# Recurrent layer of a hybrid decoder: operand tiles of two blocks, chunk steps without GpSimd

## The chip, the cores and the metric

The kernel runs on one core of one Trainium2 chip. The metric is the device time of one execution in microseconds (us), lower is better. The engines are TensorE (PE, matmuls), VectorE (DVE), ScalarE (ACT), GpSimd (POOL) and SyncE (SP, which here only issues DMAs). SBUF is the on-chip memory, PSUM holds the results of matmuls.

## The reference

The program is a decoder of two layers on one sequence of 512 tokens with 1024 channels, all in float32. Layer 0 is sparse attention with an MLP; layer 1, which the change concerns, is an RWKV-7 mixer with an MLP. Cut to what matters:

```python
# per token t, 16 heads of 64 channels: r, w (decay), k, v, kk, b = kk * a
sa    = einsum('bhvk,bhk->bhv', state, -kk_t)
state = state * w_t + sa[..., None] * b_t + v_t[..., None] * k_t
y     = einsum('bhvk,bhk->bhv', state, r_t)
# after the scan, per head:
mean = mean(y); var = mean((y - mean)**2)
y = (y - mean) * rsqrt(var + LNX_EPS) * lnx_w + lnx_b
bonus = sum(r * k * r_k) * v
out = ((y + bonus) * g) @ w_o
```

## The kernel before, in words

Channels lie on partitions in 8 blocks of 128 (two heads each), tokens on the free axis. Large matmuls are made with operands split in a high and a low part (`hi`, `lo`, three products in `gemm`, lines 119 to 121); a weight block of 1 MB for two blocks is loaded to `wraw` by a DMA on SP (line 76) and split by ACT (line 93) and DVE (line 101).

The scan runs over 8 chunks of 64 tokens. Its stages in `rwkv`:

- *Middle* (m = 0 to 7): per block, `front` and `middle` make the chunk operands. `AR` holds for each block and chunk the pair (a, r), `KB` the pair (b, k); each is 4 tiles, two for chunks 0 to 3 and two for chunks 4 to 7, of four blocks each (`half(t, f)` is one half of the tokens). `back` makes the 64x64 matrices `Mt` of all chunks, `rhat` the r operand, `bonus` sums over a head. The r GEMMs run between them.
- *Inversion* (`invert`): the diagonal 32x32 blocks of all the chunks' matrices go through DRAM (`dn`) into `tn`, one matrix per partition and half f, and are inverted in 30 iterations, each a product and an add for each half (lines 1030, 1033). Then a transposed copy `tt`, stores to DRAM (`dm`, `dt`), and loads into `Mt` and `T11`. `invert` is a generator: it yields an estimate of cost, and `run(t)` takes pieces up to t; HOLD (1e9) ends a call.
- *v GEMM*: per weight block, with `run(RUNW)` in between; `vcopy` brings v to `VT`, one tile per four chunks.
- *Chunk steps* n = 0 to 7: `step_z` multiplies the operand AL and the state-and-value tile `SV` (line 1323) and copies to `Zb`; `step_u` multiplies by the inverse and copies into `SV`; `step_n` makes the next state (L1350, `st`, `sv` L1357, `Sb`, `sn`); `step_r` and `step_y` make the output. Beside them run, for the next chunk, `acopy` (a part of AL, GpSimd), `vload` (values into `SV`, GpSimd), `opnd` (masked products into AL and `BL`, transposes), `merge` (the off-diagonal part of the inverse), and for chunks before, `gnorm` (group norm) and `turn` (transposes). `vmean` takes the mean of v beforehand, and `vload` subtracts it. The gate GEMM (`g2`), the split of the layer's output (`out`) and the output projection (`wo`) are pulled in at written places (`fill`).

Large tiles come from one pool of 21 slots (tag `b8`); a slot is free when the last reader of its tile is done. A planner orders the instructions of each engine by their place in the program and by priorities (`PR`, a number of places by which a site is put earlier; `gnorm` has 200, `step_u` 400, `acopy` 400, `vload` -100, `step_r` -1000) and its own costs. In the loop of chunk steps PE is taken out of it: `manual_schedule` keeps PE's instructions as written. Each engine executes its queue in order.

Of the kernel before, what the change touches and what calls it, by code (L numbers as in the profile page):

```python
# [765 lines left out]
def rwkv(c, x, ks, gi):  # L766
# [155 lines left out]
    KB, Mt = [[], []], []  # L922
    pc = c.tmp.tile([128, KC, NCH], F32, name="pc", tag="pc", bufs=1)

    def kb(f, m, s):
        return KB[f][m // 4][:, m % 4, :, s]
# [3 lines left out]
    pbo = pb[:, 0, :64].rearrange("p (n a e) -> p n a e", n=NCH, e=2)  # L930

    @c.site("front")
    def front(m):
# [20 lines left out]
    def middle(m):  # L954
        if m % 4 == 0:
            for f in range(2):
                KB[f].append(c.b8("KB", F32, (128, 4, 4, 2, 64)))
# [15 lines left out]
        for f in range(2):  # L973
            nc.vector.scalar_tensor_tensor(kb(f, m, 0), half(bt, f), 0.5, half(iP, f), op0=OP.mult, op1=OP.mult)
        for f in range(2):
            k4 = half(kk, f)
            nc.vector.scalar_tensor_tensor(ar(f, m, 0)[:, :, 1:], k4[:, :, 1:], -1.0, ar(f, m, 1)[:, :, :63],
                                           op0=OP.mult, op1=OP.mult)
            nc.scalar.activation(ar(f, m, 0)[:, :, 0:1], k4[:, :, 0:1], AF.Copy, scale=-1.0)
# [27 lines left out]
    def invert():  # L1007
# [37 lines left out]
        yield HOLD  # L1045
# [54 lines left out]
    nc.vector.tensor_copy(bo, pbo.rearrange("p n a e -> p n (a e)"))  # L1100
# [8 lines left out]
    def sl(t, n, q):  # L1109
        return t[n // 4][q // 4][:, q % 4, n % 4]  # L1110
# [69 lines left out]
    def opl(n, j):  # L1180
# [18 lines left out]
        for e in range(2):  # L1199
            mask((j, 1, e), BL[n][:, e, js, 0:64], pl[:, e, :, 1], kon[:, None, 1].to_broadcast([128, 4, 64]))  # L1200
# [429 lines left out]
```

## Time and profile before

| | |
|---|---|
| times of three runs | 1377.22, 1379.87, 1380.18 us (median 1379.87) |
| profiled execution | 1377.53 us, span 1375.4 us |
| granted TensorE clock, mean | 0.972 |
| PE busy | 1298.9 us (94%), 8237 instructions |
| DVE busy | 805.9 us (59%), 1498 instructions |
| ACT busy | 604.9 us (44%), 1053 instructions |
| POOL busy | 190.2 us (14%), 212 instructions |
| chain of work that ended last | PE 75%, DVE 18%, ACT 3%, issue 2%, POOL 1%, DMA 1% |

The span runs from the first to the last instruction. Busy is the time in which an engine executes, without waits. The chain of work that ended last is followed back from the last instruction, at each step to what released it. In a timeline, a row has the start, the time and the engine, the line, the instruction with output and inputs, their shapes and a count; what stands in brackets at its end is the idle time of the engine before it and what ended it.

### The profile page before, as it was taken

To read this page: it belongs to the slowest core of one execution; us is meant where nothing else is said; L and a number is where in the kernel's file an instruction comes from. 1 tells how busy PE (TensorE), PEld (TensorE's weight loads), DVE (VectorE), ACT (ScalarE), POOL (GpSimd) and SP (SyncE) were. 2 spreads that over 40 slices of the span, in tenths; PEclk is the share of its full clock that TensorE was granted. 3 is DMA by queue.
4 is the path that set the end of the run, shared out by engine and by line. 5 is a ranking of instruction groups with operands and counts; after the bars stand their busy time and mean duration, and the time that the engine had idled before them with its cause. 6 is when DMAs were issued, how large, how long until landed. Compare 5 with 4: busy or idle time off the path is not lost.

```text
span 1375.4 us, 20172 instructions
## 1 busy us (share of the span) xinstructions
PE 1298.9 (94%) x8237; PEld 1063.2 (77%) x8237; DVE 805.9 (59%) x1498; ACT 604.9 (44%) x1053; POOL 190.2 (14%) x212
## 2 busy tenths in 40 slices
PE   7989899999999999999999796878999999999997
PEld 6756566888888888899567684767988888888887
DVE  5689983544422445338888897687765532245422
ACT  5545593433311334227775445665544421134421
POOL 0385650000000000000000002564220000000000
PEclk9999999999999999999999897988999999999998
DMA  7100004222333124303211235112522222322401
GB/s 287 62 31 31 1 23 162 100 65 89 100 114 114 71 92 142 133 31 123 93 59 46 66 107 101 60 39 91 184 96 88 92 92 93 122 92 81 165 1 62
DMA packets 54716, 123.86 MB, mean 90 GB/s; under 512 B 23392, under 2 KB 26080, under 8 KB 53856
## 3 DMA queue, kind: packets, MB, share of 16 engines
q1 hardware_dynamic: 52384, 120.33, 26.4%
q10 hardware_dynamic: 2240, 2.24, 0.5%
q8 instruction: 65, 1.06, 0.3%
q14 instruction: 27, 0.22, 0.1%
HBM read 115.74 MB, written 6.82 MB: 89 GB/s over the span
## 4 chain that ended last, share of the span: by engine, by line
PE 75%; DVE 18%; ACT 3%; issue 2%; POOL 1%; DMA 1%; SPq 0%; DVEq 0%; ACTq 0%; POOLq 0%
PE g L119 20%; PE g L120 20%; PE g L121 20%; DVE w L101 2%; PE g L628 2%; DVE rot L411 1%; DVE pr L1030 1%; DVE tn L1033 1%; PE d L613 1%; DVE xm L733 1%; DVE acc L497 1%; PE g L1323 1%; DVE L L587 1%; DVE m L495 1%; DVE sv L1357 1%
## 5 line engine op out<-in xcount | busy, mean ns | idle before, releaser
L101 DVE TENSOR_TENSOR w<-wraw,w 128x1024 fp32r<-128x1024 f32 x189 | 231.1, 1246 | 112.4 <-ACT w L93 112.1
L93 ACT ACTIVATE w<-wraw 128x1024 fp32r<-128x1024 f32 x198 | 201.4, 1049 | 140.8 <-DMA wraw<-in_wblk 104.5
L119 PE MATMUL g<-sh,w 128*128 128x512 f32 (+1 forms) x608 | 216.8, 357 | 0.0
L120 PE MATMUL g<-sl,w 128*128 128x512 f32 (+1 forms) x608 | 216.4, 356 | 0.0
L121 PE MATMUL g<-sh,w 128*128 128x512 f32 (+1 forms) x608 | 216.4, 356 | 0.0
L119 PE MATMUL g<-ah,w 128*128 128x512 f32 x512 | 200.6, 392 | 0.0
L120 PE MATMUL g<-al,w 128*128 128x512 f32 x512 | 200.0, 391 | 0.3 <-DVE al L257 0.3
L121 PE MATMUL g<-ah,w 128*128 128x512 f32 x512 | 199.9, 390 | 0.0
L273 ACT ACTIVATE sh<-r 128x512 fp32r<-128x512 f32 x64 | 40.4, 632 | 227.1 <-DVE r L271 227.1
L119 PEld LDWEIGHTS g<-sh,w 128*128 128x128 f32 x608 | 115.0, 189 | 16.3
L121 PEld LDWEIGHTS g<-sh,w 128*128 128x128 f32 x608 | 115.0, 189 | 16.2
L120 PEld LDWEIGHTS g<-sl,w 128*128 128x128 f32 x608 | 115.0, 189 | 16.1
L119 PEld LDWEIGHTS g<-ah,w 128*128 128x128 f32 x512 | 96.6, 189 | 20.4 <-ACT ah L256 0.4
L120 PEld LDWEIGHTS g<-al,w 128*128 128x128 f32 x512 | 96.6, 189 | 20.3 <-DVE al L257 0.6
L121 PEld LDWEIGHTS g<-ah,w 128*128 128x128 f32 x512 | 96.5, 188 | 20.1
L271 DVE SCALAR_TENSOR_TENSOR r<-g,rstd 128x512 f32<-128x512 f32 x64 | 44.1, 691 | 96.8 <-PE g L121 84.5
L275 DVE TENSOR_TENSOR sl<-q,sh 128x512 fp32r<-128x512 f32 x64 | 44.4, 693 | 75.1 <-ACT q L274 75.1
L295 DVE TENSOR_TENSOR x<-g,x 128x512 f32<-128x512 f32 x26 | 18.0, 692 | 107.6 <-PE g L121 107.6
L179 ACT ACTIVATE sq<-x 128x256 f32<-128x256 f32 (+1 forms) x56 | 26.7, 499 | 106.0 <-DVE x L295 57.2
L920 POOL MEMSET seg<- 128x512 f32 x1 | 0.5, 527 | 488.5 <-PE g L914 488.5
L597 ACT ACTIVATE L<-L,st 128x256 f32<-128x256 f32 (+3 forms) x64 | 35.1, 552 | 16.6 <-DVE st L595 16.6
L274 ACT ACTIVATE q<-r 128x512 f32<-128x512 f32 x64 | 39.4, 615 | 0.0
(314 smaller groups left out, 2501.2 us busy)
## 6 DMA issues: line engine op xcount, KB each, us to landing
wraw<-in_wblk SPq DMA_DIRECT2D x98, 1024.0 KB, 4.9
wraw<-in_wblk SPq DMA_DIRECT2D x5, 512.0 KB, 6.1
x<-in_xT SPq DMA_DIRECT2D x8, 256.0 KB, 5.3
x<-in_xT SPq DMA_DIRECT2D x2, 1024.0 KB, 6.7
xs<-x SPq DMA_DIRECT2D x2, 1024.0 KB, 4.9
x<-xs SPq DMA_DIRECT2D x2, 1024.0 KB, 4.8
dn<-Mt SPq DMA_DIRECT2D x16, 64.0 KB, 2.1
tn<-dn SPq DMA_DIRECT2D x2, 512.0 KB, 4.8
```

The source lines that it names most:

```text
L93: s.wsp = s.nc.scalar.activation(hi, r, AF.Copy)
L101: s.nc.vector.tensor_sub(out, a, b)
L119: s.nc.tensor.matmul(p, whi[:, kc, :], ahi, start=first and kc == 0, stop=False)
L120: s.nc.tensor.matmul(p, whi[:, kc, :], alo, start=False, stop=False)
L121: s.nc.tensor.matmul(p, wlo[:, kc, :], ahi, start=False, stop=last and kc == KC - 1)
L179: nc.scalar.activation(sq, xk, AF.Square)
L271: nc.vector.scalar_tensor_tensor(r, p, 0.0, rstd, op0=OP.max, op1=OP.mult)
L273: nc.scalar.activation(hi, r, AF.Square)
L274: nc.scalar.activation(q, r, AF.Square)
L275: nc.vector.tensor_sub(lo, q, hi.bitcast(F32))
L597: nc.scalar.activation(L[g][:, :n], L[g][:, :n], AF.Exp, bias=nmx[:, g:g + 1], scale=0.125, accum_out=sm[:, g:g + 1])
L628: nc.tensor.matmul(po[HF[e]], v[sc // 2][:, j:j + 64], st8[tb, pr, e][:, sc], start=sc == 0, stop=sc == tb)
```

## The change

Operand tiles: `AR` and `KB` become four tiles each of two blocks and all eight chunks, and the instructions that were made once per half of the tokens are made once per block. The copies out of PSUM alternate between ACT and DVE by block. `lwl` has full height and four tiles. `bonus` makes 4 matmuls of 128 tokens per block in place of 8 of 64, and four copies to `bo` in place of one. The inversion handles both halves in one instruction, the transposing copy goes to ACT, and two of its holds become 1. `acopy` and `vload` become DMAs on SP within SBUF. `vmean` is gone; `gnorm` subtracts the mean, and all its work is on DVE and ACT. The low parts in `out` and of the projection's weights are all made by DVE. The copies to `BL` (64x512) and `Mt` go to ACT (`TE`, `ME`). `step_r` stands before `step_u`, and the written order of PE (`manual_schedule`) is gone.

```diff
-    def half(t, f):
-        return t[:, f * 256:(f + 1) * 256].rearrange("p (n i) -> p n i", i=64)
-
-    AR = [[c.b8("AR", F32, (128, 4, 4, 2, 64)) for _ in range(2)] for _ in range(2)]
-
-    def ar(f, m, s):
-        return AR[f][m // 4][:, m % 4, :, s]
+    def chunks(t):
+        return t.rearrange("p (n i) -> p n i", i=64)
+
+    AR = [c.b8("AR", F32, (128, 2, NCH, 2, 64)) for _ in range(4)]
+
+    def ar(m, s):
+        return AR[m // 2][:, m % 2, :, s]
 
     sqs = {}
     for m in EVO:
-        nc.scalar.activation(ar(0, m, 0), half(ps[m], 0), AF.Copy)
-        nc.vector.tensor_copy(ar(1, m, 0), half(ps[m], 1))
+        if m % 2:
+            nc.vector.tensor_copy(ar(m, 0), chunks(ps[m]))
+        else:
+            nc.scalar.activation(ar(m, 0), chunks(ps[m]), AF.Copy)
...
-    lwl = [c.t("lwl", F32R) for _ in range(2)]
+    lwl = [[c.t("lwl", F32R) for _ in range(2)] for _ in range(2)]
     for i in range(2):
         nc.scalar.activation(lwh[:, i], raw[i], AF.Copy)
         for j in range(2):
             cs = slice(j * 512, (j + 1) * 512)
-            nc.vector.tensor_sub(lwl[j][E2[i]], raw[i][E2[i], cs], lwh[E2[i], i, cs].bitcast(F32))
+            nc.vector.tensor_sub(lwl[i][j], raw[i][:, cs], lwh[:, i, cs].bitcast(F32))
...
-        for f in range(2):
-            nc.vector.scalar_tensor_tensor(half(kk, f), half(prn, f), c.vec[:, KKV, m:m + 1], ar(f, m, 0),
-                                           op0=OP.mult, op1=OP.mult)
+        nc.vector.scalar_tensor_tensor(chunks(kk), chunks(prn), c.vec[:, KKV, m:m + 1], ar(m, 0), op0=OP.mult, op1=OP.mult)
...
-        for f in range(2):
-            nc.vector.tensor_mul(half(kt, f), ar(f, m, 0), half(kt, f))
-            nc.vector.tensor_mul(kb(f, m, 1), half(kt, f), half(iP, f))
+        nc.vector.tensor_mul(chunks(kt), ar(m, 0), chunks(kt))
+        nc.vector.tensor_mul(kb(m, 1), chunks(kt), chunks(iP))
...
     @c.site("bonus")
     def bonus(m):
-        for n in range(NCH):
-            nc.tensor.matmul(pbo[E2[m % 2], n, m // 2], rk[m][:, n * 64:(n + 1) * 64], rk2[:, m], start=True, stop=True)
+        for n in range(NCH // 2):
+            nc.tensor.matmul(pbo[:, n, m // 2, m % 2], rk[m][:, n * 128:(n + 1) * 128], rk2[:, m], start=True, stop=True)
...
@@ -1024,25 +1016,23 @@
         pr = [c.t("pr") for _ in range(2)]
         for k in range(30, 0, -1):
             nr = 31 - k
-            sh = [128, k, nr]
-            pv = [v[:, :k * nr].rearrange("p (a b) -> p a b", a=k) for v in pr]
-            for f in range(2):
-                nc.vector.tensor_mul(pv[f], tn[:, f, 0:k, k:k + 1].to_broadcast(sh),
-                                     tn[:, f, k:k + 1, k + 1:].to_broadcast(sh))
-            for f in range(2):
-                nc.vector.tensor_add(tn[:, f, 0:k, k + 1:], tn[:, f, 0:k, k + 1:], pv[f])
+            sh = [128, 2, k, nr]
+            pv = pr[k % 2][:, :2 * k * nr].rearrange("p (f a b) -> p f a b", f=2, a=k)
+            nc.vector.tensor_mul(pv, tn[:, :, 0:k, k:k + 1].to_broadcast(sh),
+                                 tn[:, :, k:k + 1, k + 1:].to_broadcast(sh))
+            nc.vector.tensor_add(tn[:, :, 0:k, k + 1:], tn[:, :, 0:k, k + 1:], pv)
             yield 4 * (k * nr * 1.04 + 65)
         tt = c.b8("tt", F32, (128, 2, 32, 32))
         for f in range(2):
             nc.vector.memset(tn[:, f].rearrange("p i j -> p (i j)")[:, 0:1024:33], 1.0)
-            nc.vector.tensor_copy(tt[:, f], tn[:, f].rearrange("p i j -> p j i"))
-        yield HOLD
+            nc.scalar.activation(tt[:, f], tn[:, f].rearrange("p i j -> p j i"), AF.Copy)
+        yield 1
         for f in range(2):
             nc.sync.dma_start(dm[f].rearrange("e b h i j -> (e b h) (i j)"), tn[:, f].rearrange("p i j -> p (i j)"))
             for e in range(2):
                 nc.sync.dma_start(dt[f, e].rearrange("h i j -> h (i j)"),
                                   tt[e * 64:e * 64 + 32, f].rearrange("p i j -> p (i j)"))
-        yield HOLD
+        yield 1
...
     bo = c.tmp.tile([128, NCH, 8], F32, name="bo", tag="bo", bufs=1)
-    nc.vector.tensor_copy(bo, pbo.rearrange("p n a e -> p n (a e)"))
+    for b in range(2):
+        for s in range(2):
+            nc.vector.tensor_copy(bo[E2[b], s::2].rearrange("p n (a e) -> p n a e", e=2), pbo[E2[s], :, :, b])
...
     def acopy(n):
         AL[n] = al[:, n % 2]
         for e, r in enumerate(E2):
-            for j in range(2):
-                dst, src = AL[n][r, 4 * j:4 * j + 4, e], AR[n // 4][j][r, :, n % 4, 0]
-                if n < 1:
-                    nc.scalar.activation(dst, src, AF.Copy)
-                else:
-                    nc.gpsimd.tensor_scalar(dst, src, 1.0, 0.0, op0=OP.mult, op1=OP.add)
+            for j in range(4):
+                nc.sync.dma_start(AL[n][r, 2 * j:2 * j + 2, e], AR[j][r, :, n, 0])
...
         for e in range(2):
             o = E2[1 - e]
             mask((j, 0, e), AL[n][o, js, e], pl[o, e, :, 0], kon[o, None, 0].to_broadcast([64, 4, 64]))
-        for e in range(2):
-            mask((j, 1, e), BL[n][:, e, js, 0:64], pl[:, e, :, 1], kon[:, None, 1].to_broadcast([128, 4, 64]))
+        mask((j, 1), BL[n][:, :, js, 0:64], pl[:, :, :, 1], kon[:, None, None, 1].to_broadcast([128, 2, 4, 64]))
...
     @c.site("vload")
     def vload(n):
         SV[n] = sv[:, n % 2]
         for e in range(2):
-            o = E2[1 - e]
             for b in range(2):
-                nc.gpsimd.tensor_tensor(par(SV[n][:, e])[o, :, b], VT[n // 4][E2[b], n % 4, :, e * 64:e * 64 + 64],
-                                        vm[E2[b], n, e::2, None].to_broadcast([64, 4, 64]), op=OP.add)
+                nc.sync.dma_start(par(SV[n][:, e])[E2[1 - e], :, b], VT[n // 4][E2[b], n % 4, :, e * 64:e * 64 + 64])
 
     w0 = None
     fill()
-    vmean(0)
     vload(0)
-    for n in range(1, VMN):
-        vmean(n)
...
     def step(n):
         py = step_z(n)
+        step_r(n, py)
         yield
         step_u(n)
-        step_r(n, py)
         yield
...
         y = YY[n]
         y3 = y.rearrange("p (q i) -> p q i", i=64)
         st = c.tmp.tile([128, 2, 8], F32, name="gst", tag="gst", bufs=2)
-        pool = () if n == NCH - 1 else GP
+        nc.vector.tensor_reduce(st[:, 0], y3, XS, OP.add)
+        nc.vector.tensor_scalar(st[:, 0], st[:, 0], -1.0 / 64, None, op0=OP.mult)
+        nc.vector.tensor_tensor(y3, y3, st[:, 0, :, None].to_broadcast([128, 8, 64]), op=OP.add)
         sq = c.t("sq")
         nc.scalar.activation(sq, y, AF.Square, scale=0.125)
+        bv = c.t("bv")
+        b3 = bv.rearrange("p (q i) -> p q i", i=64)
+        nc.vector.tensor_mul(b3, VT[n // 4][:, n % 4].rearrange("p a (e i) -> p (a e) i", e=2),
+                             bo[:, n, :, None].to_broadcast([128, 8, 64]))
         nc.vector.tensor_reduce(st[:, 1], sq.rearrange("p (q i) -> p q i", i=64), XS, OP.add)
         rs = rsqrt(c, st[:, 1], 8, 64e-5, OP.add)
-        (nc.gpsimd if 1 in pool else nc.vector).tensor_tensor(y3, y3, rs[:, :, None].to_broadcast([128, 8, 64]), op=OP.mult)
-        eng = nc.vector if n == NCH - 1 else nc.gpsimd
-        eng.tensor_tensor(y3, y3, lnw, op=OP.mult)
-        bv = c.t("bv")
-        b3 = bv.rearrange("p (q i) -> p q i", i=64)
-        nc.gpsimd.tensor_mul(b3, VT[n // 4][:, n % 4].rearrange("p a (e i) -> p (a e) i", e=2),
-                             bo[:, n, :, None].to_broadcast([128, 8, 64]))
-        eng.tensor_tensor(y, y, bv, op=OP.add)
+        nc.vector.tensor_tensor(y3, y3, rs[:, :, None].to_broadcast([128, 8, 64]), op=OP.mult)
+        nc.vector.tensor_tensor(y3, y3, lnw, op=OP.mult)
+        nc.vector.tensor_tensor(y, y, bv, op=OP.add)
...
-            c.split((hi[:, q], lo[:, q]), t, q % OP2 == 1 if f else q % 2)
+            c.split((hi[:, q], lo[:, q]), t, False)
...
-        c.lo_pool = f and m % LP == 1
         c.gemm(p, c.wget(WA), o[f])
...
-    with c.tc.manual_schedule(engines={mybir.EngineType.PE}):
-        for n in range(NCH):
-            s = step(n)
...
+    for n in range(NCH):
+        s = step(n)
...
-LP = 2
-OP2 = 1
-RUNW = 4750
+RUNW = 5700
...
-TE = (1, 0)
+TE = (0, 0)
 UE = (0, 0, 0, 0)
-ME = (0, 0, 1, 1)
+ME = (0, 0, 0, 0)
```

## Rows read from the trace of the kernel before

**Rows 1.** Busy time by stretch: bounds, length, then engines with instructions; PEclk; DMA.
```profile
880.00:920.00 40.00, 32.40 (x724) 28.17 (x720) 29.66 (x63) 23.55 (x48) 25.37 (x33) 0.96 0.16 55
960.00:1000.00 40.00, 38.71 (x382) 37.95 (x381) 31.11 (x56) 24.94 (x42) 7.62 (x5) 1.00 0.46 159
```

**Rows 2.** Timeline of PE, end of step 3 and start of step 4.
```profile
898.30 1.16 PE L1350 MATMUL g<-sv,BL 128*64 128x64 f32 x32
...
904.38 0.30 PE L1323 MATMUL g<-sv,abd 128*64 128x64 f32 x2 [2.49 <-DVE sv L1357]
905.41 0.80 PE L1323 MATMUL g<-sv,abd 128*64 128x64 f32 x20 [0.73 <-DVE sv L1357]
```

**Rows 3.** Timeline of DVE in step 3.
```profile
891.77 0.99 DVE L1362 TENSOR_TENSOR sn<-st,pc 128x512 f32<-128x512 f32 x1
893.65 0.68 DVE L1117 COPY BL<-d 64x512 f32<-64x512 f32 x1 [0.88 <-ACT BL L1207]
...
896.40 0.69 DVE L1393 TENSOR_REDUCE gst<-sq 128x8 f32<-128x512 f32 x1 [0.53 <-ACT sq L1392]
...
898.65 0.20 DVE L236 RECIPROCAL rsq<-rsq 128x8 f32<-128x8 f32 x1 [1.35 <-ACT rsq L235]
...
901.71 0.83 DVE L1117 COPY Mt<-g 32x256 f32<-32x256 f32 x2
902.58 0.69 DVE L1355 TENSOR_TENSOR st<-g,sn 128x512 f32<-128x512 f32 x1
903.30 1.96 DVE L1357 TENSOR_TENSOR sv<-st,pc 64x512 f32<-64x512 f32 x2
```

**Rows 4.** Timeline of PE at four other places: `bonus`, merge 0, step 2, first projection block.
```profile
785.70 1.09 PE L992 MATMUL d<-rk,rk 128*64 128x2 f32 x16
...
852.01 1.03 PE L1145 MATMUL g<-Mt,sa 32*32 32x32 f32 x30 [1.14 <-DMA Mt<-dm]
...
882.04 1.09 PE L1339 MATMUL g<-bd,Mt 128*64 128x128 f32 x16
...
949.74 0.58 PE L119 MATMUL g<-oh,w 128*128 128x256 f32 x1
```

**Rows 5.** Timeline of DVE in the middle stage, block 7.
```profile
776.21 0.69 DVE L987 TENSOR_TENSOR rk<-g,kt 128x512 f32<-128x512 f32 x1
776.81 0.69 DVE L972 SCALAR_TENSOR_TENSOR bt<-ta,kk 128x512 f32<-128x512 f32 x1
...
778.18 0.76 DVE L969 TENSOR_TENSOR KB<-kt,iP 128x256 f32<-128x256 f32 x2
778.85 0.76 DVE L974 SCALAR_TENSOR_TENSOR KB<-bt,iP 128x256 f32<-128x256 f32 x2
```

**Rows 6.** Timeline of DVE in the inversion: alone, in pairs, last copy.
```profile
799.67 0.32 DVE L1030 TENSOR_TENSOR pr<-tn 128x150 f32<-128x150 f32 x1
800.02 0.32 DVE L1033 TENSOR_TENSOR tn<-tn,pr 128x150 f32<-128x150 f32 x1
...
834.72 0.45 DVE L1030 TENSOR_TENSOR pr<-tn 128x150 f32<-128x150 f32 x2
835.08 0.45 DVE L1033 TENSOR_TENSOR tn<-tn,pr 128x150 f32<-128x150 f32 x2
...
840.06 1.04 DVE L1038 COPY tt<-tn 128x1024 f32<-128x1024 f32 x1
```

**Rows 7.** Timeline of SP's queue, loads after the inversion.
```profile
851.54 1.27 SPq L1050 DMA_DIRECT2D T<-dt  x2
```

**Rows 8.** Timeline of POOL beside the end of step 3.
```profile
903.08 3.68 POOL L1297 TENSOR_TENSOR sv<-VT,vm 64x256 f32<-64x256 f32 x4
```

**Rows 9.** Timeline of DVE in step 6, `sv` with no POOL instruction beside it.
```profile
956.79 1.40 DVE L1357 TENSOR_TENSOR sv<-st,pc 64x512 f32<-64x512 f32 x2
```

**Rows 10.** Timeline of ACT in step 2, the `bd` copies.
```profile
878.45 1.21 ACT L1119 ACTIVATE bd<-g 64x512 f32<-64x512 f32 x2
```

**Rows 11.** Waits of SP's queue, 840 to 1000 us: in total, times, longest.
```profile
SPq L1428 <- DVE w L101: 33.2, 2, 27.2
```

More of the change, by code (lines that the diff above doesn't have):

```diff
@@ L921, in rwkv, with kb @@
     nc.gpsimd.memset(seg.rearrange("p (n i) -> p n i", i=64)[:, :, 0:1], 0.0)
-    KB, Mt = [[], []], []
+    KB, Mt = [], []
     pc = c.tmp.tile([128, KC, NCH], F32, name="pc", tag="pc", bufs=1)
-    def kb(f, m, s):
-        return KB[f][m // 4][:, m % 4, :, s]
+    def kb(m, s):
+        return KB[m // 2][:, m % 2, :, s]
     fr, kts = {}, {}
     pb = c.bank2()
-    pbo = pb[:, 0, :64].rearrange("p (n a e) -> p n a e", n=NCH, e=2)
+    pbo = pb[:, 0, :64].rearrange("p (n a b e) -> p n a b e", n=NCH // 2, b=2, e=2)
     @c.site("front")
@@ L937, in front @@
         for i in range(2):
-            r = E2[i]
             nc.tensor.matmul(p[:, i], lwh[:, i, ms], wa[i], start=True, stop=False)
-            nc.tensor.matmul(p[:, i], lwl[m // 4][r, m % 4 * 128:m % 4 * 128 + 128], wa[i][r], start=False, stop=True)
+            nc.tensor.matmul(p[:, i], lwl[i][m // 4][:, m % 4 * 128:m % 4 * 128 + 128], wa[i], start=False, stop=True)
         nc.scalar.activation(th, p[:, 0], AF.Tanh, scale=0.5, bias=hv[:, 0, m:m + 1])
@@ L954, in middle @@
     def middle(m):
-        if m % 4 == 0:
-            for f in range(2):
-                KB[f].append(c.b8("KB", F32, (128, 4, 4, 2, 64)))
+        if m % 2 == 0:
+            KB.append(c.b8("KB", F32, (128, 2, NCH, 2, 64)))
         cs, ta, kk = fr.pop(m)
@@ L960, in middle @@
         iP = c.t("iP")
-        for f in range(2):
-            nc.scalar.activation(ar(f, m, 1), half(cs, f), AF.Exp)
+        nc.scalar.activation(ar(m, 1), chunks(cs), AF.Exp)
         nc.scalar.activation(iP, cs, AF.Exp, scale=-1.0)
-        nc.scalar.activation(pc[:, m], cs.rearrange("p (n i) -> p n i", i=64)[:, :, 63], AF.Copy, scale=1.0 / 16)
+        nc.scalar.activation(pc[:, m], chunks(cs)[:, :, 63], AF.Copy, scale=1.0 / 16)
         kt = c.t("kt")
         nc.scalar.activation(kt, ta, AF.Identity, scale=hv[:, 2, m:m + 1], bias=hv[:, 3, m:m + 1])
-        for f in range(2):
-            nc.vector.tensor_mul(half(kt, f), ar(f, m, 0), half(kt, f))
-            nc.vector.tensor_mul(kb(f, m, 1), half(kt, f), half(iP, f))
+        nc.vector.tensor_mul(chunks(kt), ar(m, 0), chunks(kt))
+        nc.vector.tensor_mul(kb(m, 1), chunks(kt), chunks(iP))
         kts[m] = kt
@@ L972, in middle @@
         nc.vector.scalar_tensor_tensor(bt, ta, 1.0, kk, op0=OP.add, op1=OP.mult)
[L973 to L979, printed above, removed]
+        nc.vector.scalar_tensor_tensor(kb(m, 0), chunks(bt), 0.5, chunks(iP), op0=OP.mult, op1=OP.mult)
+        k8 = chunks(kk)
+        nc.vector.scalar_tensor_tensor(ar(m, 0)[:, :, 1:], k8[:, :, 1:], -1.0, ar(m, 1)[:, :, :63], op0=OP.mult, op1=OP.mult)
+        nc.scalar.activation(ar(m, 0)[:, :, 0:1], k8[:, :, 0:1], AF.Copy, scale=-1.0)
     @c.site("rhat")
@@ L983, in rhat @@
         p = pr.pop(m)
-        for f in range(2):
-            nc.vector.tensor_mul(ar(f, m, 1), half(p, f), ar(f, m, 1))
+        nc.vector.tensor_mul(ar(m, 1), chunks(p), ar(m, 1))
         rk[m] = c.t("rk")
@@ L1000, in back @@
             for e, r in enumerate(E2):
-                nc.tensor.matmul(p[r, n], kb(n // 4, m, 0)[r, n % 4], ar(n // 4, m, 0)[r, n % 4], start=True, stop=True)
+                nc.tensor.matmul(p[r, n], kb(m, 0)[r, n], ar(m, 0)[r, n], start=True, stop=True)
         for f in range(2):
@@ L1109, in sl @@
     def sl(t, n, q):
-        return t[n // 4][q // 4][:, q % 4, n % 4]
+        return t[q // 2][:, q % 2, n]
     top = [slice(e * 64, e * 64 + 32) for e in range(2)]
@@ L1282, in rwkv @@
     sv = c.b8("sv", F32, (128, 2, 2, 8, 64))
-    vm = c.tmp.tile([128, NCH, 8], F32, name="vm", tag="vm", bufs=1)
-    @c.site("vmean")
-    def vmean(n):
-        nc.vector.tensor_reduce(vm[:, n], VT[n // 4][:, n % 4].rearrange("p a (e i) -> p (a e) i", e=2), XS, OP.add)
-        nc.vector.tensor_scalar(vm[:, n], vm[:, n], -1.0 / 64, None, op0=OP.mult)
     @c.site("vload")
@@ L1444, in rwkv @@
         fill()
-    with c.tc.manual_schedule(engines={mybir.EngineType.PE}):
-        for n in range(NCH):
-            s = step(n)
-            op, mg = iter(()), iter(())
-            if n + 1 < NCH:
-                if n + 1 >= VMN:
-                    vmean(n + 1)
-                vload(n + 1)
-                mg = merge(n + 1)
-                if n:
-                    op = opnd(n + 1)
-            for i in range(3):
-                next(s)
-                next(op, None)
-                if i < 2:
-                    next(mg, None)
-                if i == GN and n:
-                    gnorm(n - 1)
-                if i == TN and n >= TD:
-                    turn(n - TD)
-                    if n - TD == 3:
-                        out(0)
-                if 3 * n + i in PFS:
-                    c.prefetch(PFA)
-                fill()
+    for n in range(NCH):
+        s = step(n)
+        op, mg = iter(()), iter(())
+        if n + 1 < NCH:
+            vload(n + 1)
+            mg = merge(n + 1)
+            if n:
+                op = opnd(n + 1)
+        for i in range(3):
+            next(s)
+            next(op, None)
+            if i < 2:
+                next(mg, None)
+            if i == GN and n:
+                gnorm(n - 1)
+            if i == TN and n >= TD:
+                turn(n - TD)
+                if n - TD == 3:
+                    out(0)
+            if 3 * n + i in PFS:
+                c.prefetch(PFA)
+            fill()
     gnorm(NCH - 1)
@@ L1502 @@
 SNP = False
-GP = ()
 PFS = (12,)
@@ L1506 @@
 ZE = 0
-VMN = 2
 MP = ()
-TE = (1, 0)
+TE = (0, 0)
 UE = (0, 0, 0, 0)
-ME = (0, 0, 1, 1)
+ME = (0, 0, 0, 0)
 EVO = (0, 1, 2, 3, 4, 5, 6, 7)
```

2 lines of the change are left out of this document (removed).

## The prediction

> **What bounds the kernel now.** I read the busy shares by stretch first, because the whole-span share of TensorE (PE, 94%) hides where it idles. Right behind the recurrent layer's chunk steps PE is nearly full: 38.71 of 40 us between 960 and 1000 us. Inside them it is not: 32.40 of 40 us between 880 and 920 [rows 1]. So the change, which rewrites these steps, is worth what it does to PE's idle time there; PE's own work hardly changes.
>
> Next I read PE's timeline in step 3. PE has done its part by 901.9 us and then waits 2.49 and 0.73 us for VectorE's (DVE) `sv` before the next state product (L1323) runs on at 905.41 [rows 2]. Then DVE's own rows: from `sn` at 891.77 to that point it is 13.6 us. DVE starts `st` at 902.58, although the product (L1350) that `st` adds ends at about 899.5 [rows 2, 3]: until then it works through its queue of mask multiplies, copies to `BL` and `Mt` and the group norm of the step before. Two holes in the queue are printed, 0.88 us for ScalarE's (ACT) copy and 1.35 us for its square root [rows 3]; with a few smaller ones DVE is idle some 2.8 us and busy some 10.7. An ordinary step is therefore bound by DVE's queue, through the chain `st`, `sv`, next state product. ACT feeds it twice on the way (`bd`, `sv`) but is busy for only 23.55 of 40 us [rows 1].
>
> Ahead of the steps lies the inversion, which runs on DVE and then goes through DRAM; merge 0 waits for its loads until 852.01 [rows 4].
>
> **The change part by part.** The sum is made against the profiled execution, 1377.53 us (span 1375.4, so 2.1 us around it); the median of the three runs shown is 1379.87, 2.3 more.
>
> *Middle stage.* Six pairs of 128x256 DVE instructions per block become one of 128x512 each. Two halves start 0.67 us before what follows them, a 128x512 starts 0.60 us before it: 0.07 saved per pair, 0.42 per block, 3.4 over eight blocks [rows 5]. PE waits for DVE only in the last blocks, where no r GEMM is left to fill in, so I count three: 1.3. `bonus` has half as many matmuls: 16 instructions take 1.09 [rows 4], so at most 0.5 is saved per block, and nothing if a matmul with twice the stationary columns takes twice as long; I take 0.15 per block, 1.2. Value -2.5; ends -6 (all 3.4 and half of the 4) and 0. The `bo` copies (four for one) and the full-height `lwl` (as many instructions as before) lie beside idle DVE: 0, or +0.6 if they don't.
>
> *Inversion.* 120 instructions become 60 of twice the length, each of which needs the one before. The trace shows both kinds: alone and dependent, 150 elements start 0.35 us apart; as pairs of independent halves two take 0.36, 0.18 each [rows 6]. At 1.04 ns per element (150: 0.156) that is 0.20 fixed against 0.02; for the larger pairs about 0.06. The 30 iterations have 4960 elements per half and operation: merged, 60 x 0.20 + 4 x 5.16 = 32.6 us; as perfect pairs 120 x 0.06 + 20.6 = 27.8. That would be +4.8; but about 24 of the 120 ran alone before, at 0.14 more each (3.4), so I take +1, with ends of -2 (weight splits and mixes between them hide the dependence) and +5. The transposing copy `tt` (1.04 us on DVE [rows 6]) goes to ACT: the first half's copy leaves DVE's queue (-1), but both now follow the end of the inversion (+1.5): +0.5. The shorter holds (1 for HOLD, 5700 for 4750) put the same instructions earlier in the planner's order; only DVE's queue is ahead of them: 0.
> The Trainium skill, in "VectorE: DVE Perf Modes" (Rules for kernel authors), says to minimise the count of chained DVE instructions rather than semaphores, since the pipeline empties after each in any case. By that rule 60 fewer instructions would gain 60 x 0.06 = 3.6 us instead of losing 1, and the sum would be 4.6 lower; the pairs of rows 6 speak against it.
>
> *DMAs in place of GpSimd.* `acopy` is 8 DMAs of 32 KB per chunk, `vload` 4 of 64 KB, all in SP's queue. SP issues two of the inversion's loads in 1.27 us, 0.6 each [rows 7], so 12 are up to 7 us of a 13.6 us step. In an ordinary step that is hidden: values are asked for one step ahead. At the start it is not free: `vload(0)` and `acopy(1)` share SP with the loads for which merge 0 waits. All 12 ahead of them: +7; all while SP only waits for the inversion: 0. I take +1.
>
> *Chunk steps.* Per step DVE loses the `BL` copy 0.68, the two `Mt` copies 0.83, 0.13 by joining the `BL` masks (two pairs at the 0.07 above) and the stretching of instructions with two SBUF inputs beside GpSimd: the `sv` pair takes 1.96 next to GpSimd's four loads of 3.68 and 1.40 elsewhere, `sn` 0.99 against the 0.69 of `st` [rows 3, 8, 9]. That is 0.68 + 0.83 + 0.13 + 0.56 + 0.30 = 2.5. It gains the mean (reduction 0.69, a small one of 0.2, subtraction 0.69) and three products or sums that GpSimd did, 0.69 each by the reduction's and `st`'s rows: 3.6. Net +1.1 per step. Does it show? The holes could swallow it: if the added work fills the 2.8 us of holes down to 1, a step gains 0.7 instead. But the mean comes ahead of the square, so the group norm's own chain is 1.6 us longer before it reaches the square root; the group norm's priority (200) sets its last three instructions before `st`; and ACT gets three copies, 0.6 + 2 x 0.38, beside the `bd` and `sv` copies. I leave the holes as they are: +1.1, times the six steps with both a group norm and a next step, 6.7. Ends -6 (-1 per step) and +13 (ACT's 1.35 on the chain in most steps as well). `vmean` goes away (8 reductions), but these lay beside the inversion's DMAs: 0, or -2.
> The Trainium skill's "SBUF — State Buffer" (The single rule) has VectorE and GpSimd block each other for a whole instruction when both read SBUF through the shared ports. Three such DVE instructions, each behind a GpSimd one of 0.92, would be 2.8 per step instead of 0.86, and a step would come out 0.8 shorter instead of 1.1 longer; rows 3, 8 and 9 show stretching by 0.3, not a full block.
>
> *Tiles.* Before, two `AR` and two `KB` tiles hold chunks 0 to 3 alone and come free after step 3. Afterwards all eight hold every chunk and stay until steps 6 and 7: four slots fewer, of 21, for the output projection's weights, its split input and the residual. Now PE runs projection blocks from 949.74 on, inside steps 6 and 7 [rows 4]. If they start after these, both steps idle like step 3 (3.2 us each, 6.4). Half of that, +3; ends 0 (the slots suffice) and +8 (a first weight that is late as well).
>
> *Free order on PE.* No row shows it. In step 2 the written order keeps `u` (L1339) until 882.04, behind gate GEMMs, though its `bd` copies end at 879.7 [rows 4, 10]: up to -4 for two such steps. A planner that guesses wrong puts a long GEMM ahead of a state product: up to +6. I take 0, nearest to step 3, where PE's order costs little.
>
> *Weight splits and `ol`* off GpSimd: eight more DVE instructions after 940, beside less stretching: 0, or +2.
>
> Sum: -2.5 + 1.5 + 1 + 6.7 + 3 + 0 = +9.7, so 1387.2 for a profiled execution and 1389.6 against the median. About 0.2% (2.8 us) is what can be told from no change.
>
> **Rivals.**
> *Faster: GpSimd's absence is what counts.* One mechanism, in the steps: 2.5 us leave DVE's chain and the added 3.6 fall into its holes. Then `st` comes after 9.3 us of queue and 1 us of holes, 0.5 earlier than now, and `sv` is 0.56 shorter: -1.05 per step, -6.5; with -2.5 from the middle stage and -2 from `u` no longer behind gate GEMMs, -11: 1369. It decides where the holes fall below 1.7 us. For it: there are holes in every step; against: they are waits for ACT, which gets more to do.
> *Much slower: SP's queue.* SP waits in order; the residual's load stood at its head for up to 27.2 us until a slot came free [rows 11]. If a `vload` or `acopy` stands behind such a head, the next state product waits for the rest of a step, some 4 us; four of these in steps 4 to 7 on top of the sum: 1405. For it: fewer slots make such heads likelier; against: the planner orders by its own model of when slots come free.
> *No change.* The holes swallow the added DVE work but no more, and the slots suffice: -2.5 + 1.5 + 1 + 0 + 1 = +1: 1381.
>
> **Chances.** Forecast (+3 to +16) 45%, much slower 18%, faster 25%, no change 12%: so slower by over 0.2% 63%, within it 12%, faster 25%. The range reaches into the faster rival and to the queue's price, 1372 to 1407; the forecast's own is 1383 to 1396.
>
> **What would show it.** The steps' period, from the starts of L1323: 14 us and more if right, under 13 if the faster rival holds. DVE's rows between two `sv` pairs: some 11.8 us busy, holes near 2.8; `sv` pairs of 1.40 everywhere. Inversion instructions 0.2 us plus 1.04 ns per element apart. The first projection GEMM after step 6. A `vload` waiting in SP behind a weight load marks the second rival. I am wrong if DVE's holes close, or if PE's new order fills its waits with other GEMMs.

## The result and the profile after

The changed kernel takes 1392.65 us (median of 4 runs, 1391.11 to 1395.71), the kernel before 1379.54 beside it: ratio 1.0103, 95% interval 1.0089 to 1.0117, so some 14 us or 1% slower. The profiled execution took 1391.11 us, its span 1389.3. The forecast was 1389.6 with a range of 1372 to 1407. The sum came out; most of its terms did not, and the largest losses stand where I had put one microsecond or less.

Columns below are those of the rows ahead of the prediction. First the stretch from 880 to 920 us of the kernel after, then its steps 2 and 3, cut at the first product of each step (L1298); in the second fence steps 3 and 4 of the kernel before.

```profile
880.00:920.00 40.00, 36.31 (x645) 27.18 (x647) 26.96 (x59) 23.36 (x48) 0.00 (x0) 0.93 0.29 61
...
887.20:905.10 17.90, 17.06 (x328) 13.26 (x327) 11.87 (x26) 11.21 (x23) 0.00 (x0) 1.00 0.22 35
905.10:927.90 22.80, 20.48 (x298) 15.56 (x300) 14.82 (x28) 12.46 (x24) 0.00 (x0) 0.70 0.27 68
```
```profile
890.90:904.40 13.50, 10.19 (x269) 9.06 (x269) 10.29 (x23) 8.64 (x19) 8.64 (x12) 1.00 0.25 87
904.40:921.40 17.00, 11.86 (x268) 10.49 (x268) 13.41 (x25) 9.76 (x19) 11.59 (x14) 0.86 0.04 6
```

Against [rows 1], PE is busier in the steps (36.31 against 32.40 of 40 us) and DVE is less so (26.96 against 29.66). In step 3 (905 to 928) PE is busy for 20.48 of 22.8 us at a granted clock of 0.70; before, step 3 took 13.5 us at full clock, with PE waiting for a quarter of it. So the added DVE work, my main term, is not what made the steps long.

Where did the time go? Three places, each measured from one mark: a matmul pair of the norm ahead of the layer, which the change leaves alone (L206, at 605.52 us before and 603.62 after):

- The first v GEMM of the layer starts 176.5 us behind that mark before (781.99) and 167.1 after (770.75). The middle stage gained 9.4 us.
- Step 0's products end 249.4 us behind it before (854.94) and 263.3 after (866.95). So 23.3 us are lost between the start of the v GEMM and the end of these products.
- Step 7 starts 357.7 (963.2) and 375.2 (978.8) us behind it. From the end of step 0's products to there another 3.6 are lost.

Most of the loss lies between the inversion and step 0. This is ACT in the kernel before, ACT in the kernel after, PE's longest wait after (total, times, longest), then SP after:

```profile
826.00 6.24 ACT L1240 ACTIVATE VT<-d 64x256 f32<-64x256 f32 x16 [5.74 <-PE d L1224]
832.26 6.31 ACT L1240 ACTIVATE VT<-g 64x256 f32<-64x256 f32 x16
```
```profile
830.66 3.76 ACT L1028 ACTIVATE tt<-tn 128x1024 f32<-128x1024 f32 x2 [28.83 <-DVE tn L1023]
838.35 2.00 ACT L93 ACTIVATE w<-wraw 128x1024 fp32r<-128x1024 f32 x2 [3.92 <-DMA wraw<-in_wblk]
840.38 6.23 ACT L1227 ACTIVATE VT<-d 64x256 f32<-64x256 f32 x16
846.63 6.36 ACT L1227 ACTIVATE VT<-g 64x256 f32<-64x256 f32 x16
```
```profile
PE d L1182 <- ACT VT L1227: 25.1, 2, 24.0
```
```profile
830.66 0.33 SPq L1031 DMA_DIRECT2D dm<-tn  x1
831.09 0.38 SPq L76 DMA_DIRECT2D wraw<-in_wblk  x1
...
849.53 0.56 SPq L1284 DMA_DIRECT2D lnw<-in_lnw  x1
850.53 4.01 SPq L1276 DMA_DIRECT2D sv<-VT  x6
```

The v GEMM ended at 819.5, but ACT copies its result to `VT` from 840.38 on: its queue holds both `tt` copies first, which wait for the inversion (28.83 us), and then the weight splits, which wait for a load that SP issues only behind the store `dm`. PE's next products wait 24.0 us for these copies. Before, ACT copied `VT` from 826.00 to 838.6, beside the inversion. The values for step 0 (L1276) are asked for at 850.53, behind all loads of the inversion.

### The profile page after: what moved, and what is told of

Its sections match the earlier page's. It is cut to its first block, busy times and chain, and to the rows that moved or that the text cites. A ratio compares the mean times of both kernels' runs of the same rounds, so it can differ in the third digit from the quotient of the medians.

```text
span 1389.3 us, 19972 instructions
## 1 busy us (share of the span) xinstructions
PE 1311.3 (94%) x8173; PEld 1070.9 (77%) x8173; DVE 795.0 (57%) x1386; ACT 616.0 (44%) x1054; POOL 111.9 (8%) x122
## 3 DMA queue, kind: packets, MB, share of 16 engines
q8 instruction: 64, 1.05, 0.3%
## 4 chain that ended last, share of the span: by engine, by line
PE 81%; DVE 10%; ACT 4%; POOL 2%; issue 2%; DMA 1%; DVEq 0%; ACTq 0%; SPq 0%; POOLq 0%
PE g L119 20%; PE g L121 19%; PE g L120 19%; PE g L628 2%; DVE w L101 1%; PE d L613 1%; DVE rot L411 1%; PE d L1182 1%; DVE pr L1021 1%; DVE tn L1023 1%; DMA wraw<-in_wblk 1%; ACT VT L1227 1%; ACT w L93 1%; DVE L L587 1%; POOL kl L99 1%
## 5 line engine op out<-in xcount | busy, mean ns | idle before, releaser
L101 DVE TENSOR_TENSOR w<-wraw,w 128x1024 fp32r<-128x1024 f32 x193 | 234.2, 1237 | 119.9 <-ACT w L93 119.5
L1182 PE MATMUL d<-AR,KB 64*64 64x128 f32 x256 | 27.5, 318 | 26.5 <-ACT VT L1227 25.1
L1182 PEld LDWEIGHTS d<-AR,KB 64*64 64x64 f32 x256 | 18.1, 154 | 30.9 <-ACT VT L1227 26.0
```

Source lines behind the costliest of these rows:

```text
L101: s.nc.vector.tensor_sub(out, a, b)
L1182: nc.tensor.matmul(pl[E2[1 - e], e, q].rearrange("p a t -> p (a t)"), k[:, 1], ar.rearrange("p a t -> p (a t)"), start=True, stop=True)
```

## Experiments

Each ratio is against the kernel before, run beside it. One thousandth is 1.38 us.

| run | median us | ratio | 95% interval |
|---|---|---|---|
| changed kernel | 1392.65 | 1.0103 | 1.0089 to 1.0117 |
| a_tt | 1392.10 | 1.0097 | 1.0069 to 1.0125 |
| a_hold | 1389.94 | 1.0085 | 1.0062 to 1.0108 |
| a_gap | 1381.93 | 1.0030 | 1.0015 to 1.0045 |
| b_tt | 1385.11 | 1.0040 | 1.0021 to 1.0059 |
| b_lwl | 1376.47 | 0.9996 | 0.9982 to 1.0011 |
| b_mid | 1369.59 | 0.9950 | 0.9931 to 0.9970 |
| a_vl | 1365.50 | 0.9922 | 0.9906 to 0.9939 |
| a_gapman | 1372.99 | 0.9969 | 0.9956 to 0.9981 |
| a_two | 1362.27 | 0.9908 | 0.9876 to 0.9940 |
| a_vlman | 1367.19 | 0.9939 | 0.9917 to 0.9962 |
| a_vlonly | 1375.42 | 0.9996 | 0.9978 to 1.0015 |
| a_gn | 1375.75 | 1.0007 | 0.9990 to 1.0024 |

**Who holds ACT: `tt`, or SP's order?** Four runs.

```diff
 a_tt:   -nc.scalar.activation(tt[:, f], ..., AF.Copy)
         +nc.vector.tensor_copy(tt[:, f], ...)
 a_hold: -yield 1 (twice) +yield HOLD; -RUNW = 5700 +RUNW = 4750
 a_gap:  both of these, on the changed kernel
 b_tt:   the first one the other way round, on the kernel before
```

> The changed kernel with the two transposing copies `tt` back on VectorE; all else as changed. Theory: the changed kernel loses some 20 us between the end of the inversion (830.6) and the first product of step 0 (860.9, 30.3 us later; before 840.0 and 850.5, 10.5 later), because ACT's queue holds `tt` ahead of the weight splits and the 32 copies to `VT`. Then that stretch shrinks to about 13 us and the time is near 1375. Rival: what holds ACT is not `tt` but the second weight load, which SP issues only behind the inversion's store; then ACT still waits for it, the stretch stays near 29 us and the time near 1391.

> The changed kernel with HOLD twice and RUNW 4750 as before, `tt` still on ACT. SP now has both weight loads ahead of the inversion's store; ACT has its first `tt` between the two weight splits, the second after seven copies to `VT`. Theory (ACT's queue): the stretch from the end of the inversion to step 0 stays near 28 us, 1390. Rival (SP's order): it shrinks to about 13, 1375.

> The changed kernel with both undone: `tt` on VectorE, HOLD twice, RUNW 4750. Both theories: the stretch is near 12 us, and with a middle stage some 9 us shorter the time is near 1373. If the loss lies in the chunk steps instead, 1388 or more.

> The kernel before with `tt` on ACT alone. SP's order stays as before; ACT has a `tt` between the weight splits and one after 17 copies to `VT`. ACT's-queue theory: the copies to `VT` wait for the end of the inversion (840) instead of starting at 826, step 0 starts some 10 us later, 1390. SP's-order rival: no change, 1380.

ACT's rows in a_tt, then in a_hold, then in b_tt:

```profile
838.38 2.00 ACT L93 ACTIVATE w<-wraw 128x1024 fp32r<-128x1024 f32 x2 [35.86 <-DMA wraw<-in_wblk]
```
```profile
830.82 1.94 ACT L1028 ACTIVATE tt<-tn 128x1024 f32<-128x1024 f32 x1 [27.67 <-DVE tn L1023]
832.66 1.04 ACT L93 ACTIVATE w<-wraw 128x1024 fp32r<-128x1024 f32 x1
833.72 2.71 ACT L1227 ACTIVATE VT<-d 64x256 f32<-64x256 f32 x7
```
```profile
836.12 1.96 ACT L1038 ACTIVATE tt<-tn 128x1024 f32<-128x1024 f32 x1 [21.36 <-DVE tn L1033]
837.97 1.05 ACT L93 ACTIVATE w<-wraw 128x1024 fp32r<-128x1024 f32 x1
839.04 6.23 ACT L1240 ACTIVATE VT<-d 64x256 f32<-64x256 f32 x16
```

In a_tt the rival came true (ACT waits 35.86 us for the load), in a_hold the theory did (with the load in place ACT waits 27.67 for the inversion). So each of the two holds ACT by itself, and taking one away gives next to nothing: 1 and 2.5 us, within the intervals. Taken away together they give 10 us (1.0103 to 1.0030). b_tt confirms it from the other side: step 0 starts 9.2 us later than before (859.8), of which 5.5 are left in the time.

a_gap was expected near 1373 and took 1382. In it, SP still asks for the values behind 16 loads of the inversion, and PE waits for them at step 0:

```profile
853.34 0.45 PE L1298 MATMUL g<-sv,abd 128*64 128x64 f32 x2 [2.98 <-DMA sv<-VT]
853.72 1.07 PE L1127 MATMUL g<-T,Mt 32*32 32x32 f32 x32
```

**The value loads.** a_vl copies the values with GpSimd on top of a_gap; a_vlonly does so on the changed kernel and leaves all else.

```diff
-nc.sync.dma_start(par(SV[n][:, e])[E2[1 - e], :, b], VT[...])
+nc.gpsimd.tensor_scalar(par(SV[n][:, e])[E2[1 - e], :, b], VT[...], 1.0, 0.0, op0=OP.mult, op1=OP.add)
```

> a_gap with the values copied into `sv` by GpSimd (four copies per chunk) instead of four DMAs. Theory: in a_gap, SP issues the DMAs for chunk 0 at 849.1 behind the inversion's 24 DMAs, so step 0 starts 5 us after merge 0 and the planner puts the operands of chunk 1 among its products (853.3 to 859.0); without that step 0 ends near 852, 1375. Rival: GpSimd's copies stretch VectorE's `sv` from 1.41 to near 1.9 in most steps, and the steps give it back: 1381.

> The changed kernel with only the value loads taken from the DMA queue and given to GpSimd (four copies per chunk); `tt` on ACT, the shorter holds and RUNW 5700 as changed. Theory: two causes add up: the value loads cost some 16 us (1381.9 to 1365.5 without the queue effect), the stall of ACT behind the inversion some 10; here only the second is left: 1376. Rival: step 0 still waits for the late copies to `VT` (853), so the values come no earlier than before and little is gained: 1388 to 1392.

a_vl gave 10 us more than expected, 15 against a_gap; a_vlonly came as its theory said, 15 below the changed kernel. So the two causes add up: 15 us for the loads as they are made here, 10 for ACT's stall. These are steps 1 to 3 of a_vlonly (windows as above) and GpSimd's rows in a_vl:

```profile
865.40:881.50 16.10, 15.62 (x276) 11.74 (x274) 8.28 (x20) 11.92 (x23) 1.34 (x4) 1.00 0.11 19
881.50:897.20 15.70, 15.15 (x274) 10.96 (x273) 12.56 (x25) 9.60 (x21) 2.60 (x4) 1.00 0.12 19
897.20:908.80 11.60, 11.20 (x242) 8.86 (x240) 8.97 (x20) 8.62 (x19) 1.61 (x4) 1.00 0.15 25
```
```profile
821.62 5.34 POOL L1276 TENSOR_SCALAR sv<-VT 64x256 f32<-64x256 f32 x8 [1.49 <-ACT VT L1227]
...
855.05 1.84 POOL L1276 TENSOR_SCALAR sv<-VT 64x256 f32<-64x256 f32 x4 [15.74 <-PE g L1344]
```

Step 3 takes 11.6 us at full clock instead of 22.8 at 0.70; as PE's order moves work between steps, steps 1 to 3 together are the better measure: 43.4 us instead of 54.5. The two kernels differ in one statement, yet PE's order differs: in step 3 of the changed kernel PE goes from `u` through operand products and transposes of a later chunk (L1182, L1183, L1193) before it comes to step_n's product (L1325), 6 us after `u` has ended; in a_vlonly that product follows `u` within 0.7 us. PE first waits 0.96 us for `sv`, then 1.18 for DVE's masks, and soon after its granted clock is at the lower of its two levels (0.50, which is 1.2 of 2.4 GHz) from about 914 to 928. That PE's new order fills its waits with other products is what the prediction named as a sign of being wrong. In order: `u` and step_n's product in the changed kernel, the same in a_vlonly, the second wait, and then the windows.

```profile
909.91 1.09 PE L1314 MATMUL g<-bd,Mt 128*64 128x128 f32 x16
917.17 1.33 PE L1325 MATMUL g<-sv,BL 128*64 128x64 f32 x18
```
```profile
900.71 1.09 PE L1314 MATMUL g<-bd,Mt 128*64 128x128 f32 x16
902.36 0.33 PE L1325 MATMUL g<-sv,BL 128*64 128x64 f32 x2
```
```profile
913.25 0.29 PE L1182 MATMUL d<-AR,KB 64*64 64x128 f32 x1 [1.18 <-DVE BL L1177]
```
```profile
908.00:912.00 4.00, 3.86 (x103) 3.10 (x94) 3.35 (x7) 2.40 (x6) 0.00 (x0) 1.00 0.28 45
912.00:916.00 4.00, 2.82 (x17) 1.54 (x16) 3.49 (x11) 2.24 (x6) 0.00 (x0) 0.78 0.55 138
916.00:920.00 4.00, 4.00 (x47) 2.94 (x49) 0.45 (x1) 0.42 (x1) 0.00 (x0) 0.50 0.38 153
```

That the planner expects a DMA's values later than a copy's, and so fills PE's queue with other work, is read from these orders, not measured. The next pair of runs bears on it.

**The free order.** a_gapman and a_vlman are a_gap and a_vl with the order of PE's instructions in the steps written out again.

```diff
+with c.tc.manual_schedule(engines={mybir.EngineType.PE}):
+    for n in range(NCH):   # and step_r after step_u again
```

> a_gap with TensorE's written order for the chunk steps, as in the kernel before. Theory: the free order costs (in step 4 of the changed kernel VectorE waits 5.16 us for the product of `step_n`, behind operand, merge and transpose products): steps 1 to 7 in some 100 us instead of 103.8, 1378. Rival: the free order fills waits with other products; without it 1385 or more.

> a_vl with TensorE's written order for the chunk steps. Theory: a free order is good where the values are there early and bad where the planner sees them late: with the values copied by GpSimd steps 1 to 7 take 97 us in the free order; in the written one some 101, 1369. Rival: the written order is as good or better here too, as it was by 9 us on a_gap: 1357 to 1365.

| | values by DMA | values by GpSimd |
|---|---|---|
| free order | 1.0030 (a_gap) | 0.9922 (a_vl) |
| written order | 0.9969 (a_gapman) | 0.9939 (a_vlman) |

a_gapman gained more than expected (1373.0 against 1378), a_vlman came near its theory (1367.2 against 1369). In the written order the DMAs cost some 4 us (0.0030, and the intervals overlap), in the free one 15. The free order loses 8 us with DMAs; with copies it is some 2 us ahead, within the intervals. So of the loads' 15 us, about 4 are the loads and 11 are what the free order makes of them.

**The middle stage.** b_lwl is one edit on the kernel before, b_mid all of the middle stage and its tiles.

```diff
 b_lwl: -lwl[m // 4][r, ...], wa[i][r]      +lwl[i][m // 4][:, ...], wa[i]
 b_mid: b_lwl, bonus in 64 matmuls, merged instructions, AR and KB in tiles
        of two blocks, joined BL masks, acopy by DMA
```

> The kernel before with `lwl` at full height (128 rows, zeros of the other operand's rows kept in `wa`) and nothing else. Theory: in the kernel before, the 16 matmuls of 64 rows in `front` and the full-height ones beside them stand 0.33 to 0.43 us apart, full-height ones after the change 0.23; so 0.6 us per block on TensorE, which has nothing else to hide it behind: the v GEMM starts near 777 instead of 782 and the time is near 1374. Rival (my prediction's step): it lies beside other work, 1379.

> The kernel before with the changed tiles and middle stage (operands in tiles of two blocks, merged instructions, full-height `lwl`, `bonus` in 64 matmuls), the joined `BL` masks and `acopy` by DMA; inversion, value loads, group norm and PE order as before. Theory: all of the gain of the change is here and the tiles cost nothing later: the v GEMM starts near 772, step 0 near 845, time near 1370. Rival (tiles): the missing slots delay the output weights, first projection block after 950, and steps 6 and 7 give back 3 to 8 us: 1376.

The theory of b_lwl fell: it was to give 5 us, and the v GEMM came 0.9 us nearer the mark (175.5 against 176.5). The rows in question did move. In the kernel before (first fence, with a window) a matmul of half height and the one behind it start 0.43 us apart, in b_lwl (second fence), with full height, 0.23:

```profile
751.53 0.50 PE L940 MATMUL d<-wa,lwl 64*128 64x512 f32 x1
751.96 0.50 PE L939 MATMUL d<-wa,lwh 128*128 128x512 f32 x1
752.39 0.49 PE L940 MATMUL d<-wa,lwl 64*128 64x512 f32 x1
...
720.00:760.00 40.00, 39.94 (x307) 28.41 (x307) 32.20 (x70) 20.32 (x42) 0.00 (x0) 1.00 0.24 64
```
```profile
750.76 0.39 PE L939 MATMUL d<-wa,lwh 128*128 128x512 f32 x1
750.98 0.39 PE L940 MATMUL d<-wa,lwl 128*128 128x512 f32 x1
751.21 0.39 PE L939 MATMUL d<-wa,lwh 128*128 128x512 f32 x1
```

Counted from start to start, these 32 matmuls take 3.2 us less of PE in b_lwl, but up to the last r GEMM PE then idles 1.9 us more, in waits for DVE of up to 1.26 us. So the saving on PE shows only where DVE is shortened as well.

b_mid has the whole gain of the stage (167.1 us from the mark, as in the changed kernel) and 7 us of time. It does not keep all of it: from the start of step 1 to that of step 7 it takes 107.0 us against 100.2, with step 2 at a clock of 0.72. How the 9.4 divide between the edits of the stage was not tried; the traces give the following. Of the 9.4, 7.3 are gained before the last r GEMM ends, where PE is full. From start to start the matmuls of `lwh` and `lwl` take 4.0 us less there, the r GEMMs between them 1.9, `bonus` 0.8, and PE's waits 0.8. The last blocks, where PE waits for DVE, give 2.0.

**The group norm.** a_gn is a_vl with the means and the group norm of the kernel before.

```diff
+vmean(n) for all chunks ahead of the steps; vload: gpsimd.tensor_tensor(sv, VT, vm, op=OP.add)
-three DVE products and sums, the mean  +gpsimd.tensor_tensor / tensor_mul (3)
```

> a_vl with the group norm of the kernel before: means taken out of the values (`vmean`), added by GpSimd as the values are copied, three products and sums of the group norm on GpSimd. Theory (my prediction): VectorE's 3.6 us for these cost 1.1 us per step net, so this is 6 us faster: 1359. Rival: they fall into holes of VectorE's queue, and GpSimd's longer copies (0.92 each instead of 0.46) stretch `sv`: no faster, 1365 to 1371.

It is 12 us slower, not 6 faster. DVE's `sv` and `sn` by group, 840 to 960 us (busy us, mean ns of one), in the kernel after and then in a_gn; in a_vl the means are 691 and 804. Below the dots, DVE in step 4 of a_gn, PE's waits for `sv` (total, times, longest), its wait ahead of step 0, and step 5:

```profile
L1332 DVE TENSOR_TENSOR sv<-st,pc 64x512 f32<-64x512 f32 x10 | 6.8, 681 | 0.1
L1337 DVE TENSOR_TENSOR sn<-st,pc 128x512 f32<-128x512 f32 x5 | 3.4, 687 | 0.1
```
```profile
L1344 DVE TENSOR_TENSOR sv<-st,pc 64x512 f32<-64x512 f32 x10 | 10.7, 1069 | 0.2
L1349 DVE TENSOR_TENSOR sn<-st,pc 128x512 f32<-128x512 f32 x5 | 6.0, 1198 | 0.2
...
918.22 0.58 DVE L239 SCALAR_TENSOR_TENSOR rsq<-rsq 128x8 f32<-128x8 f32 x1
918.72 1.21 DVE L101 TENSOR_TENSOR w<-wraw,w 128x1024 fp32r<-128x1024 f32 x1
919.85 1.10 DVE L1382 TENSOR_TENSOR y<-y,rsq 128x512 f32<-128x512 f32 x1
920.88 2.35 DVE L1344 TENSOR_TENSOR sv<-st,pc 64x512 f32<-64x512 f32 x2
923.26 1.65 DVE L1349 TENSOR_TENSOR sn<-st,pc 128x512 f32<-128x512 f32 x1
...
PE g L1310 <- DVE sv L1344: 7.6, 3, 6.0
PE d L1193 <- DVE BL L1177: 5.4, 2, 5.1
...
921.80:944.00 22.20, 19.95 (x268) 14.09 (x269) 9.34 (x17) 9.05 (x19) 5.37 (x5) 0.67 0.25 68
```

Some 4 us are lost ahead of step 0, whose products end 249.3 us behind the mark instead of 245.4: all eight reductions of `vmean` stand in DVE's queue ahead of the last `BL` masks, and the transposes that need these start on PE 5.2 us later than in a_vl (238.7 against 233.5 behind the mark). Steps 1 to 3 are as in a_vl within a microsecond, though DVE has less to do (in step 2 it is busy for 9.49 us against 12.57). In step 4 the added GpSimd work stretches what stands ahead of `sv` and `sv` itself, PE waits 6.0 us for it, and step 5 then runs at 0.67 of the clock: 19.2 and 22.2 us for these two steps against 11.2 and 17.9 in a_vl.

**The inversion's halves.** a_two is a_vl with the two halves as separate instructions.

```diff
+for f in range(2): tensor_mul(pv[f], tn[:, f, ...])   # then tensor_add, per half
```

> a_vl with the inversion's two halves as separate instructions again (120 instead of 60). Theory: merged, both halves end together, and the loads of half 0, on which step 0 waits, start some 4 us later than need be; from the first store of half 0 step 0 follows by 12 to 14 us in every run. Two halves bring step 0 some 4 to 6 us nearer (in b_mid it starts 10.3 us after the inversion's end, in a_vl 14.6): 1360. Rival: the two halves cost VectorE what my prediction said they save (1 us less merged cost, 0.5 for the second copy), and step 0 does not move: 1365.

It has the best median of all, 1362.27, 0.9% below the kernel before; against a_vl the intervals overlap. Counted from the mark, the inversion ends where it did (228.9 against 228.8 us) and step 0 starts 2.8 us earlier (240.6 against 243.4), less than the 4 to 6 expected.

## Why the sum was right and its terms were not

The forecast said +9.7, and +13 to +14 was measured. That the time fell into the range is luck, since the errors of the terms cancelled. Term by term:

- **Middle stage: -2.5 (ends -6 and 0) against -9.4.** That PE waits for DVE only in the last blocks was read rightly (waits of 3.08, 2.73 and 1.27 us from 769 on), and these blocks gave 2.0 against the 1.3 that I took. `bonus` gave 0.16 per block against 0.15. The failed term is `lwl` at 0: I looked at it on DVE alone, but PE was busy for 39.94 of 40 us between 720 and 760, and up to the last r GEMM the matmuls of `lwh` and `lwl` took 4.0 us more of PE than after the change. The ends were too narrow.
- **Merged inversion: +1 against none on DVE.** The size law held: after the change 300 elements stand 0.50 us apart (0.20 + 0.31), as [rows 6] gave it. What I left out is that half 0, for which step 0 waits, no longer ends first: 2.8 us at step 0, some 2 in the time (within the intervals). The Trainium skill, in "VectorE: DVE Perf Modes" (Rules for kernel authors), says to minimise the count of chained DVE instructions. Here 60 fewer ended no sooner: 228.8 against 228.9 us.
- **`tt` and the holds: +0.5 and 0 against +10.** The failed step is "only DVE's queue is ahead of them". I priced the copy and not what is queued behind it on ACT: two weight splits and 32 copies to `VT`. For the holds I did not look at SP, where `dm` came ahead of a weight load.
- **DMAs in place of GpSimd: +1 (ends 0 and +7) against +15.** That SP asks late for chunk 0's values was foreseen; with a written order it costs some 4 with all else. The rest comes through PE's free order. I priced these two edits apart, each near nothing, and their product is the largest loss of the change.
- **Chunk steps: +6.7, and `vmean` at 0, against -12 for their main part.** The three products and the mean on DVE gain (a_gn against a_vl). The failed step is "I leave the holes as they are: +1.1, times the six steps": in steps 1 to 3 the added work fell into the holes, and in sum nothing shows. Some 4 of the 12 are `vmean`, which did not lie hidden beside the DMAs; the rest is one event, in steps 4 and 5. So the faster rival had the sign and the holes right, but its gain of 1.05 in every step is not seen. Nor do the periods of the steps decide between the two, as I had meant them to: in the kernel after they go from 12.1 us (step 4) to 25.9 (step 6). I had the stretching per step at 0.86 us from [rows 3, 8, 9]; that is about what left (`sv` from 966 to 681 ns and `sn` from 933 to 687 on average between the two kernels, 0.82 per step). But a_gn shows where it bites: in one step it adds up to a 6 us wait of PE, behind which the next step ran at 0.67 of the clock. The Trainium skill, in "SBUF — State Buffer" (Who interferes with whom), has a DVE instruction with two SBUF inputs contend with a GpSimd one that reads SBUF. The trace agrees: `sn` takes 1198 ns on average in a_gn, 0.5 us above its 687 without GpSimd, and up to 1.65 us, where I took 0.3 more.
- **Tiles: +3, not seen.** The first projection block still runs in step 6 (965.7 us, between 952.9 and 978.8; in b_mid 939.67, between 926.9 and 953.6). Whether the tiles are behind b_mid's longer steps is open.
- **Free order: 0 (ends -4 and +6) against +8 with DMAs, about -2 with copies.**

The slower rival did not occur as described: between 840 and 985 us none of PE's waits in the changed kernel names a value load (two at L1298, 1.8 us in all, have no cause in the trace), and SP's longest one at such a load (L1276, 14.9 us) is for the buffer that step_z's products still read.

A chain of runs covers the whole way (in us, from the ratios): the kernel before to b_mid -7, b_mid to a_gn +8, a_gn to a_vl -12, a_vl to a_vlonly +10, a_vlonly to the changed kernel +15; together +14. The +8 holds the merged inversion, the eight means ahead of step 0, the free order with `step_r` moved, the splits moved from GpSimd and the copies moved to ACT; these were not separated. By the traces it lies ahead of the steps: step 0's products end 10 us later from the mark (249.3 against 239.4), and from step 1 to step 7 it is 107.5 us against 107.0. So I was right on the sign and the size because two large losses, through queues, outweighed two gains that I had mis-sized by 7 and 19 us.

## What to carry over

Price a moved instruction by what stands behind it in its new queue, not by its own length: two copies of 1.9 us held up 34 others, and together with a load that SP issued late they cost 10 us. With two blockers in two queues, undoing one at a time on the changed kernel showed almost nothing; only both together, or one of them on the kernel before, did. Price a scheduler's freedom together with the way the values arrive; neither edit shows its cost alone. And where GpSimd works beside a DVE chain, count what leaves GpSimd too before counting what DVE gets: here that was worth more than the added DVE work, through one long wait.

## What was not expected of the hardware

- Short waits of PE inside a busy stretch can be followed by a long one at half clock: after waits of 0.96 and 1.18 us in step 3 the granted clock stood at 0.50 from about 914 to 928 us, and the step took 22.8 us instead of 11.6. Not every wait does this: in step 5 of a_vlonly PE idles for 4.0 of 17.5 us in all, and the granted clock stays at 1.00.
- GpSimd copies 64x256 values in 0.40 us each where nothing stretches them (a_vl, from 855 us) and the add of the mean takes 0.61 (before, at 862.9); other ones in the same runs take some 0.72 and 0.95. In a_vl, with the copies, `sv` takes 0.69 on average and `sn` 0.80.
- A matmul over 64 rows between two over 128 rows costs itself and the one behind it: starts 0.43 us apart in the kernel before, 0.23 in b_lwl, where only the height differs, both at full clock.
